# TensorE reads the two halves of its moving operand in turn

## The chip, the cores and the metric

The kernel runs on one core of a Trainium2 chip. The metric is the device time of one execution in microseconds (us). Before the change it is 957.76 us, the median of 3 runs (957.65 to 957.94).

## The reference

One layer of a pooling mixer with two RMS norms, on 4096 frames of 1024 channels in float32:

```
normed = rms_norm(h, norm_w)
u, gate = split(normed @ in_w, 2)                 # in_w: 1024 x 2048
pooled = [trailing_mean(u_g, window_g) for 4 groups, windows 2/4/8/16] - u
mixed = einsum('bsgc,gcd->bsgd', pooled, group_w) + group_b
y = mixed * scale * silu(gate)
h = h + y @ out_w                                  # out_w: 1024 x 1024
out = rms_norm(h, final_norm_w)
```

## The kernel before

The group maps are folded into the input weights at the start (`fold`, line 364), so that two large products are left: the input product, in two passes `a` and `b` over the halves of the weights, and the output product `o`. Each is done with Strassen's scheme in Winograd's form: a 2 x 2 block product by seven products P1 to P7 instead of eight. The order of the seven is `ORDER_IN` and `ORDER_OUT` (lines 32 and 33).

Each float32 operand is split in two parts by `split` (line 153): ScalarE rounds it to fp32r, VectorE subtracts that from the operand, and the rest is the second part. `mm3` (line 554) then issues three fp32r matmuls for one product of 128 x 128 by 128 x 512: first part by first, first by second, second by first. The three add up in one PSUM bank of 512 float32 columns.

There are 56 steps of the input product (2 passes, 4 blocks of 1024 frames, 7 products), each with 48 matmuls (`product_in`, line 563), and 56 of the output product (8 blocks of 512 frames, 7 products), each with 24 (`product_out`, line 584). In `product_in` the stationary operand is a slice of 128 columns of the weights `w[i][h]`, and the moving operand is a row of 512 frames of an activation tile `op`. In `product_out` the activations are stationary and a row of 512 columns of `w[i]` is moving. All matmuls of both go through `mm3`. The last step of all does its second bank as two pieces of 256 columns, the second of them into the bank called "spare", so that the tail can begin earlier.

`evict_in` (line 665) and `evict_o` (line 861) read the banks. After P1 ScalarE copies the banks into another set of banks, on which later products accumulate. The other products are copied to SBUF by ScalarE (in one case through a SiLU) or added to an SBUF tile by VectorE. In the output part the SBUF tile is the row of `x` to which the product is added; `finish` (line 763) then takes squares, the inverse root and the final weights, and stores the rows. In the last block the same is done in pieces by `square_part`, `early_half`, `late_factor`, `late_scalar` and `late_vector` (lines 797 to 859).

Eight banks serve as two sets of four in the input part and as four pairs that rotate in the output part. Loads run three to four steps ahead, forming and splitting of operands one to two steps ahead (lines 1132 to 1141 and the loop from line 1156). In the head, before the first product, TensorE runs eight constant products (line 978), the folds (line 373) and the spreading of the norm factors over a bank (line 432). `spread_rs` (line 424) reads its own bank 7 with a step of 128 words in the source (lines 442 to 445).

Of the kernel before, what the change touches and what calls it, by code (L numbers as in the profile page):

```python
# [12 lines left out]
AF = mybir.ActivationFunctionType  # L13
ALU = mybir.AluOpType
# [4 lines left out]
H = 512  # L19
# [9 lines left out]
EPS = 1e-6  # L29
# [31 lines left out]
def kernel(  # L61
# [66 lines left out]
    def take(pattern="p (a b) -> p a b", pool=None, **sizes):  # L128
        sizes = sizes or {"a": 2}
        if pool is None:  # L130
            spare = len(vt.free) > keep[0] or not st.free
            pool = vt if spare and vt.age() < st.age() else st
        return pool.take(lambda t: t[:, 0:D].rearrange(pattern, **sizes))

    def take_v():
        return vt.take(lambda t: t.rearrange("p (a b) -> p a b", a=2))
# [4 lines left out]
    def add(dst, a, b):  # L141
        nc.vector.tensor_tensor(out=dst, in0=a, in1=b, op=ALU.add)  # L142
# [4 lines left out]
    def mul(dst, a, b):  # L147
        nc.vector.tensor_tensor(out=dst, in0=a, in1=b, op=ALU.mult)  # L148

    def copy(dst, src, func=AF.Copy):  # L150
        return nc.scalar.activation(dst, src, func)  # L151
# [107 lines left out]
    parts, t2 = {}, {}  # L259
# [291 lines left out]

    def mm3(ps, lt, r, start, stop):

        for n, (a, b) in enumerate(((lt[0], r[0]), (lt[0], r[1]), (lt[1], r[0]))):
            latest[0] = nc.tensor.matmul(  # L557
                ps, a, b, start=start and n == 0, stop=stop and n == 2, skip_group_check=True
            ).ins
# [24 lines left out]
    def product_out(i, t, sets, last):  # L584
        ps = sets[bank_of[i]]
        for j in range(2):
            rows = slice(j * P, (j + 1) * P)
            size = H // 2 if last and j == 1 else H
            for c in range(0, H, size):
                cols = slice(c, c + size)  # L590
                dst = sets["spare"] if c else ps[j]
                for k in range(4):
                    wk = w[i][k // 2]
                    mm3(
                        dst[:, cols],
                        (t[:, 0, k, rows], t[:, 1, k, rows]),
                        (wk[:, 0, k % 2, cols], wk[:, 1, k % 2, cols]),
                        (i in (P1, P7) or c > 0) and k == 0,
                        k == 3,
                    )  # L600


# [59 lines left out]
    def cells(us, lo=0):  # L662
        return [us[c // 2][:, c % 2, lo:] for c in range(4)]

    def evict_in(b, q, i, sets):
        ps = sets[bank_of[i]]
        last = None
        if i == P1:
            for c in range(len(copied), 4):
                last = copy(sets["y"][c], ps[c])  # L670
            copied.clear()
        elif i == P2:
            ev["11"] = [take() for _ in range(2)]
            for c, u in enumerate(cells(ev["11"])):
                last = copy(u, ps[c], AF.Silu)
        elif i == P6:
            ev["21"] = [take() for _ in range(2)]
            for c, u in enumerate(cells(ev["21"])):
                last = copy(u, ps[c])
        elif i == P7:  # L680
            ev["22"] = [take_v() for _ in range(2)]
            for c, u in enumerate(cells(ev["22"], HIST)):
                last = copy(u, ps[c])
        elif i == P5:
            for c, u in enumerate(cells(ev["22"], HIST)):
                add(u, ps[c], u)
        elif i == P4:
            for c, u in enumerate(cells(ev["21"])):
                add(u, ps[c], u)
            for u in ev["21"]:  # L690
                copy(u, u, AF.Silu)
        else:
            ev["12"] = [take_v() for _ in range(2)]
            for c, u in enumerate(cells(ev["12"], HIST)):
                last = copy(u, ps[c])
        if last is not None:
            evicted[0] = last.ins

# [82 lines left out]
    partial = {}  # L781
# [3 lines left out]
    def column():  # L785
        k = next(free_columns)
        return columns[:, k : k + 1]

    def mean_part(ss, before):

        ms = column()
        partial["added"] = nc.vector.tensor_scalar(
            out=ms, in0=ss, scalar1=1.0 / D, scalar2=before, op0=ALU.mult, op1=ALU.add
        ).ins
        return ms

    def square_part(u):
        ss = column()
        partial["square"] = nc.scalar.activation(  # L799
            partial["junk"][:, 0, 0 : u.shape[1]], u, AF.Square, accum_out=ss  # L800
        )
        return ss

    def early_half(half, j, n):

        u = hs[NBO - 1][half, j][:, n]
        partial[half, j] = mean_part(square_part(u), EPS)
        mul(u, u, fw[0][:, n])

    def late_factor(half, j, parts):  # L810
# [26 lines left out]
    def late_scalar(half, j, n, rs, queue):  # L837
        u = hs[NBO - 1][half, j]
        with tc.issue_after(partial["last"].ins):
            partial["last"] = nc.scalar.activation(u[:, 1 - n], u[:, 1 - n], AF.Copy, scale=rs)  # L840
        partial["sent"] = queue.dma_start(
            out=out[row_of(NBO - 1, half, j), (1 - n) * H : (2 - n) * H], in_=u[:, 1 - n]
        ).ins
# [17 lines left out]
    def evict_o(b, i, sets):  # L861
        ps = sets[bank_of[i]]
        final = b == NBO - 1
        if final and i == P7:
            partial["junk"] = take()
        factors = []
        for j in range(2):
            if i == P1:
                copy(sets["y"][j], ps[j])
                continue  # L870
            half, n = {P7: (1, 1), P6: (1, 0), P2: (0, 0), P5: (1, 1), P4: (1, 0), P3: (0, 1)}[i]
            u = hs[b][half, j][:, n]
            last = final and i in (P4, P3)
            parts = 2 if last and i == P3 and j == 1 else 1
            for p in range(parts):
                c = slice(p * (H // parts), (p + 1) * (H // parts))
                src = sets["spare"] if p else ps[j]
                partial["added"] = nc.vector.tensor_tensor(  # L878
                    out=u[:, c], in0=src[:, c], in1=u[:, c], op=ALU.add
                ).ins  # L880
                if last:
                    with tc.issue_after(partial["last"].ins) if p else nullcontext():
                        partial["part", p] = square_part(u[:, c])
                if parts == 2 and p == 0:
                    partial["last"] = partial["square"]
                    late_scalar(half, 0, n, factors[0], nc.sync)
            if last:
                factors.append(late_factor(half, j, parts))
                if i == P4 and j == 1 or i == P3 and j == 0:
                    if i == P4:  # L890
                        late_scalar(half, 0, n, factors[0], nc.scalar)
                        late_vector(half, 0, n, factors[0])
                        partial["waiting"] = (half, 1, n, factors.pop())
                    else:
                        rows = partial.pop("waiting")
                        late_scalar(*rows, nc.scalar)
                        late_vector(*rows)
        if final and i == P3:
            late_vector(half, 0, n, factors[0])
            late_scalar(half, 1, n, factors[1], nc.scalar)  # L900
            late_vector(half, 1, n, factors[1], 2)
        if final and i == P5:
            u = hs[b][0, 1][:, 1]
            add(u[:, H // 2 :], ps[1][:, H // 2 :], u[:, H // 2 :])
        if final and i in (P2, P5):
            for j in range(2):
                early_half(half, j, n)
        elif not final and i in (P4, P3):
            finish(b, 1 if i == P4 else 0)
# [37 lines left out]
    def run(n, between=None, behind=None):  # L947
        kind, b, i = steps[n]
        sets = sets_of(kind, b)
        if kind == "o":  # L950
            product_out(i, split_up.pop(n), sets, n == len(steps) - 1)
            evict_o(b, i, sets)
        else:
            product_in(i, split_up.pop(n), sets, i == P1, between, behind)
            evict_in(b, 0 if kind == "a" else 1, i, sets)
# [125 lines left out]
    s = xs[0]  # L1081
# [74 lines left out]
    for n in range(2, len(steps)):  # L1156
        kind, b, i = steps[n]
# [49 lines left out]
        if kind in ("a", "b"):  # L1207
# [7 lines left out]
            if kind == "b" and b == NB - 1 and i == P3:  # L1215
                f = take("p (a b) -> p a b", a=2)
                nc.sync.dma_start(
                    out=f.rearrange("p a b -> p (a b)"), in_=final_w.partition_broadcast(P)
# [54 lines left out]
```

## Time and profile before

| | |
|---|---|
| median of 3 runs | 957.76 us (957.65 to 957.94) |
| the profiled execution | 957.33 us, span 955.5 us |
| mean granted TensorE clock | 0.998 |
| HBM read and written | 115.45 MB and 60.83 MB |
| matmul records | 4212, of which 4044 on line 557 |

In the profile PE is TensorE's matmuls, PEld its weight loads, which run beside them, DVE is VectorE, ACT ScalarE, POOL GpSimd and SP SyncE. A group of instructions shows its line, engine and operation, what it writes and reads with the shapes, the count, then the busy time in us and the mean ns of one, then the idle time of the engine before them and what ended it. A row of the timeline shows a start, a length and a number of instructions merged into it; the length reaches from the first start to the last end. A row of windows shows the stretch, its length and the busy time of PE, PEld, DVE, ACT and POOL with counts, then the granted clock, the share of the DMA engines and GB/s. A row of waits shows who waited for whom, the total in us, how often, and the longest.

### The profile page before, as it was taken

What the parts mean: (1) busy time and instruction counts of PE and PEld (TensorE: products, weight loads), DVE (VectorE), ACT (ScalarE), POOL (GpSimd) and SP (SyncE); (2) the same over time, 40 slices, a digit from 0 to 9 for tenths busy, and PEclk for the clock granted to TensorE, in tenths of its full rate; (3) what the DMA queues carried; (4) which work ended last, traced back from release to release, by engine and by line L of the source; (5) the groups of instructions that cost most, each with busy time, mean ns of one, the idle gap of its engine ahead of it and who ended that gap; (6) DMA issues with size and microseconds to landing.
All of it is one profiled execution on the core that took longest, in us unless ns stands there. A gap on an engine that the chain in (4) does not pass through costs nothing.

```text
span 955.5 us, 11153 instructions
## 1 busy us (share of the span) xinstructions
PE 947.0 (99%) x4212; PEld 784.2 (82%) x4212; DVE 731.5 (77%) x807; ACT 455.8 (48%) x685; POOL 46.4 (5%) x118
## 2 busy tenths in 40 slices
PE   9999999999999999999999999999999999999997
PEld 7888888888888888888888888888888888888886
DVE  3897984894895994796695699499977667676665
ACT  6968457447345455345345435552433424324333
POOL 0023001000000000000000000000101101001010
PEclk9999999999999999999999999999999999999999
DMA  9976666557566644018415724645746536456022
GB/s 344 402 292 241 229 239 196 193 215 245 208 243 218 211 143 143 11 57 295 154 45 195 263 93 140 221 150 172 255 155 210 165 119 222 119 188 210 32 89 89
DMA packets 67573, 177.01 MB, mean 185 GB/s; under 512 B 6720, under 2 KB 24512, under 8 KB 67520
## 3 DMA queue, kind: packets, MB, share of 16 engines
q1 hardware_dynamic: 61616, 156.37, 47.6%
q10 hardware_dynamic: 4176, 13.65, 3.7%
q0 software_dynamic: 1728, 6.29, 1.7%
q8 instruction: 33, 0.54, 0.2%
q14 instruction: 20, 0.16, 0.1%
HBM read 115.45 MB, written 60.83 MB: 184 GB/s over the span
## 4 chain that ended last, share of the span: by engine, by line
PE 95%; DMA 3%; ACT 1%; DVE 0%; SPq 0%; issue 0%; DVEq 0%; ACTq 0%
PE bank L557 94%; DMA early<-in_wut 2%; DMA st<-in_x 1%; PE bank L373 0%; ACT early L407 0%; ACT op L151 0%; ACT w L151 0%; ACT st L799 0%; ACT bank L151 0%; ACT vt L407 0%; PE bank L432 0%; SPq L342 0%; SPq L352 0%; DVE st L878 0%; ACT early L389 0%
## 5 line engine op out<-in xcount | busy, mean ns | idle before, releaser
L557 PE MATMUL bank<-op,w 128*128 128x512 f32 x2688 | 610.5, 389 | 0.2 <-ACT w L223 0.2
L557 PEld LDWEIGHTS bank<-op,w 128*128 128x128 f32 x2688 | 504.4, 188 | 105.5 <-ACT w L223 0.6
L557 PE MATMUL bank<-w,op 128*128 128x512 f32 (+1 forms) x1356 | 305.0, 387 | 0.0
L557 PEld LDWEIGHTS bank<-w,op 128*128 128x128 f32 x1356 | 253.1, 188 | 51.9
L151 ACT ACTIVATE op<-st 128x1024 fp32r<-128x1024 f32 x126 | 132.7, 1057 | 181.3 <-PE bank L557 169.3
L145 DVE TENSOR_TENSOR op<-st,op 128x1024 fp32r<-128x1024 f32 x126 | 152.8, 1219 | 70.9 <-ACT op L151 70.7
L142 DVE TENSOR_TENSOR vt<-vt 128x1028 f32<-128x1028 f32 (+6 forms) x72 | 87.4, 1228 | 0.1
L151 ACT ACTIVATE vt<-bank 128x512 f32<-128x512 f32 x102 | 59.5, 596 | 47.1 <-PE bank L557 46.6
L151 ACT ACTIVATE op<-vt 128x1024 fp32r<-128x1024 f32 x40 | 42.3, 1059 | 72.0 <-PE bank L557 72.0
L878 DVE TENSOR_TENSOR st<-bank,st 128x512 f32<-128x512 f32 x60 | 41.2, 688 | 39.5 <-PE bank L557 39.5
L145 DVE TENSOR_TENSOR st<-st,st 128x1024 f32<-128x1024 f32 x38 | 46.0, 1218 | 14.5 <-DMA st<-wvd 9.1
L145 DVE TENSOR_TENSOR op<-vt,op 128x1024 fp32r<-128x1024 f32 x40 | 48.8, 1221 | 10.1 <-ACT op L151 10.0
L151 ACT ACTIVATE bank<-bank 128x512 f32<-128x512 f32 x48 | 27.9, 581 | 38.9 <-PE bank L557 31.6
L193 POOL TENSOR_SCALAR oms<-oss 128x2 f32<-128x2 f32 x14 | 9.7, 690 | 639.5 <-ACT st L768 635.0
L878 DVE TENSOR_TENSOR vt<-bank,vt 128x512 f32<-128x512 f32 (+1 forms) x37 | 24.9, 673 | 16.1 <-PE bank L557 16.0
L142 DVE TENSOR_TENSOR vt<-bank,vt 128x512 f32<-128x512 f32 (+1 forms) x55 | 36.0, 678 | 0.3 <-PE bank L557 0.2
L145 DVE TENSOR_TENSOR w<-st,w 128x1024 fp32r<-128x1024 f32 x20 | 24.1, 1220 | 11.9 <-ACT w L151 11.7
L642 DVE SCALAR_TENSOR_TENSOR vt<-vt,vt 128x1024 f32<-128x1024 f32 x24 | 29.2, 1217 | 0.0
L151 ACT ACTIVATE w<-st 128x1024 fp32r<-128x1024 f32 x20 | 20.9, 1058 | 16.1 <-PE bank L557 15.4
L148 DVE TENSOR_TENSOR st<-st,st 128x1024 f32<-128x1024 f32 (+1 forms) x19 | 21.7, 1162 | 6.9 <-DMA st<-rd 6.2
L647 DVE SCALAR_TENSOR_TENSOR vt<-vt,colt,vt 128x512 f32<-128x512 f32 x38 | 26.8, 744 | 0.0
L772 DVE SCALAR_TENSOR_TENSOR st<-st,ors,st 128x1024 f32<-128x1024 f32 x17 | 21.4, 1281 | 6.1 <-POOL ors L211 6.1
(121 smaller groups left out, 506.4 us busy)
## 6 DMA issues: line engine op xcount, KB each, us to landing
st<-in_x SPq DMA_DIRECT2D x33, 512.0 KB, 4.6
st<-sd SPq DMA_DIRECT2D x29, 512.0 KB, 5.0
st<-in_xt SPq DMA_DIRECT2D x25, 512.0 KB, 6.5
vt<-in_x SPq DMA_DIRECT2D x24, 512.0 KB, 4.7
sd<-st ACTq DMA_DIRECT2D x19, 512.0 KB, 3.4
yd<-vt SPq DMA_DIRECT2D x19, 512.0 KB, 3.0
st<-yd SPq DMA_DIRECT2D x19, 512.0 KB, 3.8
out<-st SPq DMA_DIRECT2D x17, 512.0 KB, 4.1
```

The costliest lines, as they stand in the source:

```text
L142: nc.vector.tensor_tensor(out=dst, in0=a, in1=b, op=ALU.add)
L145: return nc.vector.tensor_tensor(out=dst, in0=a, in1=b, op=ALU.subtract)
L148: nc.vector.tensor_tensor(out=dst, in0=a, in1=b, op=ALU.mult)
L151: return nc.scalar.activation(dst, src, func)
L193: nc.gpsimd.tensor_scalar(out=ms, in0=ss, scalar1=1.0 / D, scalar2=EPS, op0=ALU.mult, op1=ALU.add)
L557: latest[0] = nc.tensor.matmul(ps, a, b, start=start and n == 0, stop=stop and n == 2, skip_group_check=True).ins
L642: nc.vector.scalar_tensor_tensor(out=s[:, :, at : at + H], in0=s[:, :, at : at + H], scalar=1.0 / win, in1=v[:, :, HIST:], op0=ALU.mult, o ...
L647: nc.vector.scalar_tensor_tensor(out=sg[:, j], in0=s[:, j, at : at + H], scalar=bias_c[2 * grp + j], in1=sg[:, j], op0=ALU.add, op1=ALU.mult,)
L772: nc.vector.scalar_tensor_tensor(out=us[j], in0=us[j], scalar=rs[:, j : j + 1], in1=fw[0], op0=ALU.mult, op1=ALU.mult,)
L878: partial["added"] = nc.vector.tensor_tensor(out=u[:, c], in0=src[:, c], in1=u[:, c], op=ALU.add).ins
```

## The change

A bank's 512 columns are held in the order 0, 256, 1, 257, ..., 255, 511. `woven` gives the moving operand in that order, as a pattern of 256 by 2 with an inner step of 256 words, so each matmul writes its bank as contiguously as before and reads its moving operand from the first and the second half in turn. `plain` reads a bank back in the old order, with a step of two words, and `halved` gives an SBUF tile the matching shape. The columns of the last step's pieces are now counted in pairs: each piece has 128 columns of either half. The copies from bank to bank after P1 keep the new order. The stationary operands, the folds and the spreading are not touched.

```
+    def halved(ap):
+        return ap.rearrange("p (s a) -> p s a", s=2)
+    def woven(ap):
+        return ap.rearrange("p (s a) -> p a s", s=2)
+    def plain(bank):
+        return bank.rearrange("p (a s) -> p s a", s=2)
-    def mm3(ps, lt, r, start, stop):
+    def mm3(bank, lt, r, start, stop, cols=slice(0, H // 2)):
+        ps = bank.rearrange("p (a s) -> p a s", s=2)[:, cols]
+        r = [woven(b)[:, cols] for b in r]
         for n, (a, b) in enumerate(((lt[0], r[0]), (lt[0], r[1]), (lt[1], r[0]))):
             latest[0] = nc.tensor.matmul(
                 ps, a, b, start=start and n == 0, stop=stop and n == 2, skip_group_check=True
...
-            size = H // 2 if last and j == 1 else H
-            for c in range(0, H, size):
-                cols = slice(c, c + size)
+            size = H // 4 if last and j == 1 else H // 2
+            for c in range(0, H // 2, size):
                 dst = sets["spare"] if c else ps[j]
                 for k in range(4):
                     wk = w[i][k // 2]
                     mm3(
-                        dst[:, cols],
+                        dst,
                         (t[:, 0, k, rows], t[:, 1, k, rows]),
-                        (wk[:, 0, k % 2, cols], wk[:, 1, k % 2, cols]),
+                        (wk[:, 0, k % 2], wk[:, 1, k % 2]),
                         (i in (P1, P7) or c > 0) and k == 0,
                         k == 3,
+                        slice(c, c + size),
                     )
...
-                last = copy(u, ps[c], AF.Silu)
+                last = copy(halved(u), plain(ps[c]), AF.Silu)
...
-                add(u, ps[c], u)
+                add(halved(u), plain(ps[c]), halved(u))
...
-            partial["junk"][:, 0, 0 : u.shape[1]], u, AF.Square, accum_out=ss
+            halved(partial["junk"][:, 0])[:, :, 0 : u.shape[2]], u, AF.Square, accum_out=ss
...
-                c = slice(p * (H // parts), (p + 1) * (H // parts))
-                src = sets["spare"] if p else ps[j]
+                c = slice(p * (H // 2 // parts), (p + 1) * (H // 2 // parts))
+                src = plain(sets["spare"] if p else ps[j])[:, :, c]
+                dst = halved(u)[:, :, c]
                 partial["added"] = nc.vector.tensor_tensor(
-                    out=u[:, c], in0=src[:, c], in1=u[:, c], op=ALU.add
+                    out=dst, in0=src, in1=dst, op=ALU.add
                 ).ins
...
-            add(u[:, H // 2 :], ps[1][:, H // 2 :], u[:, H // 2 :])
+            late = halved(u)[:, :, H // 4 :]
+            add(late, plain(ps[1])[:, :, H // 4 :], late)
```

More of the change, by code (lines that the diff above doesn't have):

```diff
@@ L678, in evict_in @@
             for c, u in enumerate(cells(ev["21"])):
-                last = copy(u, ps[c])
+                last = copy(halved(u), plain(ps[c]))
         elif i == P7:
@@ L682, in evict_in @@
             for c, u in enumerate(cells(ev["22"], HIST)):
-                last = copy(u, ps[c])
+                last = copy(halved(u), plain(ps[c]))
         elif i == P5:
             for c, u in enumerate(cells(ev["22"], HIST)):
-                add(u, ps[c], u)
+                add(halved(u), plain(ps[c]), halved(u))
         elif i == P4:
             for c, u in enumerate(cells(ev["21"])):
-                add(u, ps[c], u)
+                add(halved(u), plain(ps[c]), halved(u))
             for u in ev["21"]:
@@ L694, in evict_in @@
             for c, u in enumerate(cells(ev["12"], HIST)):
-                last = copy(u, ps[c])
+                last = copy(halved(u), plain(ps[c]))
         if last is not None:
@@ L806, in early_half @@
         u = hs[NBO - 1][half, j][:, n]
-        partial[half, j] = mean_part(square_part(u), EPS)
+        partial[half, j] = mean_part(square_part(halved(u)), EPS)
         mul(u, u, fw[0][:, n])
@@ L882, in evict_o @@
                     with tc.issue_after(partial["last"].ins) if p else nullcontext():
-                        partial["part", p] = square_part(u[:, c])
+                        partial["part", p] = square_part(dst)
                 if parts == 2 and p == 0:
```

## The prediction

> **What bounds the kernel now.** I read the busy totals first, then the chain of waits, the waits of TensorE, and a stretch in the middle.
>
> ```profile
> span 955.5 us, 11153 instructions
> PE 947.0 (99%) x4212; PEld 784.2 (82%) x4212; DVE 731.5 (77%) x807; ACT 455.8 (48%) x685; POOL 46.4 (5%) x118
> PEclk9999999999999999999999999999999999999999
> 57.59 888.62 PE bank L557 x3919
> 37.70:953.50 915.80, 911.15 (x4032) 754.36 (x4030) 710.19 (x778) 427.85 (x640) 46.02 (x113) 1.00 0.51 178
> ```
>
> TensorE is busy for 99% of the span, at the full granted clock in every slice. The fourth line, from the chain of work that ended last, says that 888.62 us of it are 3919 matmuls of line 557 in one piece. The last line, a stretch without the head, has 911.15 of 915.80 us busy.
>
> ```profile
> PE bank L373 <- DMA early<-in_group_w: 0.8, 1, 0.8
> PE bank L978 <- PEq L1258: 0.8, 1, 0.8
> PE bank L373 <- DMA early<-in_wut: 0.3, 1, 0.3
> PE bank L557 <- ACT w L223: 0.2, 1, 0.2
> ```
>
> These are all the waits of TensorE in total: 2.1 us, of which 0.2 belong to line 557. No eviction, buffer or transfer holds it. The time is therefore the number of matmuls times the distance between two of them. These rows give both.
>
> ```profile
> L557 PE MATMUL bank<-op,w 128*128 128x512 f32 x2688 | 610.5, 389 | 0.2 <-ACT w L223 0.2
> L557 PE MATMUL bank<-w,op 128*128 128x512 f32 x1332 | 302.1, 389 | 0.0
> L557 PE MATMUL bank<-w,op 128*128 128x256 f32 x24 | 3.0, 283 | 0.0
> L557 PEld LDWEIGHTS bank<-op,w 128*128 128x128 f32 x2688 | 504.4, 188 | 105.5 <-ACT w L223 0.6 <-DVE op L145 0.4
> ...
> 399.76 4.47 PE L557 MATMUL bank<-op,w 128*128 128x512 f32 x19
> ...
> 13.77 3.40 PE L373 MATMUL bank<-w,w 128*128 128x256 f32 x27
> ```
>
> The 389 ns of one is its whole passage; neighbours overlap. The distance comes from the timeline: 19 matmuls take 4.47 us, the last of them its full 0.389, so (4.47 - 0.389) / 18 = 0.2267 us for 512 columns. The 27 fp32r matmuls of 256 columns in the head, with 283 ns for the last, give (3.40 - 0.283) / 26 = 0.1199 us. The difference, 0.1068 us for 256 columns, is 0.417 ns per column, and 0.2267 - 0.2136 = 0.013 us per matmul are left that do not depend on the columns. The 0.417 ns is the speed at which moving words now arrive, every one beside its neighbour.
>
> **The change, part by part.** No instruction is added, removed or moved: the same matmuls, weight loads, evictions and DMAs in the same order. What differs is the order of addresses within them.
>
> *The moving reads.* Each of the 4020 matmuls of 512 columns and the 24 of 256 now reads word 0, word 256, word 1, word 257 and so on: every word lies about 1 KiB from the one before it (in the last step's pieces too). No read of SBUF in this trace steps like that, so the price is bounded by rows.
>
> ```profile
> L978 PE MATMUL bank<-const-bfloat16-1.0 128*128 128x512 bf16 x8 | 3.2, 572 | 0.8 <-PEq L1258 0.8
> L151 ACT ACTIVATE op<-st 128x1024 fp32r<-128x1024 f32 x126 | 132.7, 1057 | 181.3 <-PE bank L557 169.3 <-DVE st L148 8.8 <-issue 2.0
> L145 DVE TENSOR_TENSOR op<-st,op 128x1024 fp32r<-128x1024 f32 x126 | 152.8, 1219 | 70.9 <-ACT op L151 70.7
> ```
>
> The cheap end is nothing, or less (the gain is priced among the rivals). For the dear end: the other engines take a 4-byte word from SBUF in 1057 / 1024 = 1.03 ns (ScalarE) and 1219 / 1024 = 1.19 ns (VectorE). TensorE takes one in 0.417 ns, 2.5 to 2.9 times as fast. That makes it likely, though not shown, that its reader fetches neighbours together; when neighbours in time are never neighbours in place, it fetches once per word. If single words came at VectorE's pace, a matmul would cost 512 x (1.19 - 0.417) = 0.396 us more: 4020 x 0.396 + 24 x 0.198 = 1597 us, ending at 957.3 + 1597 = 2554 us. If it fetches pairs today, one word per fetch doubles the column to 0.835 ns. A row near that is TensorE's own slowest stream, the eight constant products at the start: 3.2 us / 8 / 512 = 0.78 ns per column. I take 0.835 ns, because TensorE's own row lies beside it and VectorE's time holds more than a read. The matmul then costs 0.2136 us more, 0.440 in all.
>
> [...]
>
> *The evictions.* They read PSUM with a step of two words. For ScalarE there is a row with a much longer step: the copy of bank 7 after the eight products of line 432 reads with a step of 128 words (lines 442 to 445).
>
> ```profile
> 22.68 1.19 PE L432 MATMUL bank<-w,hl 128*128 128x128 f32 x8
> 23.91 0.60 ACT L151 ACTIVATE st<-bank 128x512 f32<-128x512 f32 x1 [1.64 <-PE bank L432]
> L151 ACT ACTIVATE vt<-bank 128x512 f32<-128x512 f32 x102 | 59.5, 596 | 47.1 <-PE bank L557 46.6
> L878 DVE TENSOR_TENSOR st<-bank,st 128x512 f32<-128x512 f32 x60 | 41.2, 688 | 39.5 <-PE bank L557 39.5
> L878 DVE TENSOR_TENSOR vt<-bank,vt 128x512 f32<-128x512 f32 x35 | 24.1, 688 | 16.0 <-PE bank L557 16.0
> L142 DVE TENSOR_TENSOR vt<-bank,vt 128x512 f32<-128x512 f32 x54 | 35.6, 683 | 0.3 <-PE bank L557 0.2
> L142 DVE TENSOR_TENSOR st<-bank,st 128x512 f32<-128x512 f32 x10 | 6.7, 682 | 0.1
> 650.00:940.00 290.00, 290.00 (x1281) 240.22 (x1280) 211.69 (x243) 101.27 (x146) 22.23 (x70) 1.00 0.46 154
> ```
>
> That copy takes 0.60 us, the contiguous ones 0.596, so ScalarE's evictions cost nothing more. For VectorE no row has a step; its 60 + 35 + 54 + 10 = 159 evictions of 512 columns lie between no change and twice 0.69 us, at most 110 us in all. I take nothing, by ScalarE's row. The cover is TensorE's stream: with today's pace VectorE would go from 731.5 to 841 busy us; in the output part, the last line above, 95 of these evictions would bring it from 211.7 to 277 of 290 us, which still fits but tightly. If some evictions were then late, the next product's bank or operand would be late, and I allow up to 10 us for it. If the matmuls double, the cover doubles too. Near the end two of VectorE's are of 256 columns:
>
> ```profile
> 947.66 0.42 DVE L878 TENSOR_TENSOR vt<-bank,vt 128x256 f32<-128x256 f32 x1
> ...
> 949.18 0.41 DVE L878 TENSOR_TENSOR vt<-bank,vt 128x256 f32<-128x256 f32 x1
> ...
> L557 PE MATMUL bank<-op,w x2688: 387/389/578, 32.7 to 643.9; 128*128 128x512 f32 x192
> ```
>
> Only the second comes after the last matmul, so the tail grows by under 0.5 us even if it doubles.
>
> *Sum.* The profiled execution took 957.33 us, 1.8 more than its span, and lies 0.4 under the median of 957.76. The head, up to the first matmul of line 557 at 32.7 us (last line above), and the tail keep their time. 957.3 + 4020 x 0.2136 + 24 x 0.1068 = 957.3 + 858.7 + 2.6 = **1819 us**.
>
> **The rivals.**
>
> 1. *The hops are free* (a buffer in TensorE's reader holds both halves' words). For it: each half by itself is still read in order, so every fetched block is used up within a few columns. Against it: the reader must then serve two streams at 0.417 ns per word, and nothing here shows that it can. Time: 957.8; with late VectorE evictions up to 968.
>
> [...]
>
> 2. *Faster* (the other side): each matmul carries 0.013 us that its columns do not explain, and a weight load of 188 ns runs under it. If that is the moving stream held up by the weight load at one place of SBUF, reading two places in turn could take the delay away.
>
> ```profile
> 24.62 3.62 PE L373 MATMUL bank<-early,early 128*128 128x256 f32 x16
> L373 PE MATMUL bank<-early,early 128*128 128x256 f32 x96 | 21.7, 382 | 1.1 <-DMA early<-in_group_w 0.8 <-DMA early<-in_wut 0.3
> ```
>
> For it: the float32 products of the head, 48 in the code and 96 in the trace, stand (3.62 - 0.379) / 15 = 0.2161 us apart (0.379 is this shape's usual length); if each record streams its 256 columns twice, at half the word rate, only 0.0024 us is left, so the 0.013 is not fixed for all products. Against it: the distance is the same 0.2267 at any place and load, and a slower fetch would outweigh it. It decides from the point where hopping costs less than 0.02 ns a column. Price: 4020 x (0.2267 - 0.2161) = 43 us, so 915.
>
> 3. *A fetch brings four words*: then single words run at a quarter of the rate, three times 0.2136 more per matmul: 957.3 + 3 x 861.3 = 3541 us. For it: full-rate fp32 with a wide block needs the fewest fetches. Against it: 1.67 ns per word would be slower than VectorE's 1.19, which holds two operands and a write.
>
> 4. *A part of the hops hides*: somewhere between free and double; half of it is 1388 us.
>
> 5. *Between double and VectorE's pace*: 1819 to 2554, say 2190 us.
>
> **How the numbers follow.** Half rate 0.36; free 0.25, of which 0.19 within 0.2% (about what a measurement of this kernel can tell from no change) and 0.06 beyond it through evictions; faster 0.10; quarter rate 0.13; partly hidden 0.11; above double 0.05. Half rate leads because reading neighbours in pairs is the least that the pace ratio of the rows asks for. Faster is 0.10, same 0.19, slower 0.36 + 0.06 + 0.13 + 0.11 + 0.05 = 0.71. The range leaves out the quarter rate and half of the faster case (below 935): 935 to 2554, which holds 0.36 + 0.25 + 0.05 + 0.11 + 0.05 = 0.82. The likeliest case's own range is 1790 to 1850.
>
> **What would show it.** Right: the distance between matmuls of line 557 is 0.43 to 0.45 us, the 24 short ones double as well, the head's line 373 keeps 0.1199, and the granted clock stays at 1.00; a lower clock at the same distance would mean a throttle instead of reads. ScalarE's evictions stay near 0.60 us and VectorE's at 0.68 to 0.69. TensorE waits for nothing new, and VectorE's share falls to about 731.5 / 1817 = 40%. The forecast is wrong if the distance stays at 0.2267 (free) or nears 0.216 (faster), or if VectorE's evictions lengthen and TensorE's waits grow beyond 2 us.

## The result and the profile after

| | before | after |
|---|---|---|
| median | 957.71 us (4 runs, 957.65 to 957.94) | 924.66 us (4 runs, 922.32 to 926.86) |
| ratio, with its 95% interval | | 0.9654 (0.9622 to 0.9686) |
| the profiled execution, and its span | 957.33 us, 955.5 us | 926.72 us, 924.9 us |

The changed kernel is 3.5% faster. The forecast was 1819 us, and its range began at 935. Among all the executions that follow, one, of the version with words 4 apart, was slow (1248.68 us at a granted clock of 0.72), and its ratio leaves it out. The page of the kernel after, its totals and the row of the granted clock:

```profile
span 924.9 us, 11163 instructions
PE 907.7 (98%) x4212; PEld 791.0 (86%) x4212; DVE 729.1 (79%) x807; ACT 449.4 (49%) x685; POOL 48.9 (5%) x118
PEclk9999999999999999999999999999999999999999
```

Each engine has as many instructions as before, but TensorE is busy for 39 us less. A piece of the timeline after, in the middle, gives the distance between two matmuls (line 570 is line 557 of before):

```profile
398.69 4.48 PE L570 MATMUL bank<-op,w 128*128 128x512 f32 x20
```

With 0.379 us for the last one (the groups' rows give 379 to 381 ns of one), it is (4.48 - 0.379) / 19 = 0.2158 us, against 0.2267 before. That is 10.8 ns less on each matmul. 4020 matmuls of 512 columns make it 43.5 us, but the profiled execution gained only 30.6. The waits of TensorE after show where the rest went:

```profile
PE bank L570 <- DVE op L145: 5.5, 4, 2.5
PE bank L570 <- ACT bank L151: 1.5, 1, 1.5
PE bank L570 <- ACT w L223: 1.3, 1, 1.3
```

Line 557 had waited 0.2 us in all; line 570 waits 8.3. Summed over the trace's start times from the first product on, the distances longer than the usual one are 13.9 us over it after and 1.1 before. 43.5 - 12.8 = 30.7 us, which is the gain to 0.1 us. The first of the large waits, TensorE's timeline after, then the same stretch before:

```profile
111.71 8.15 PE L570 MATMUL bank<-op,w 128*128 128x512 f32 x37
122.33 9.94 PE L570 MATMUL bank<-op,w 128*128 128x512 f32 x37 [2.47 <-DVE op L145]
```

```profile
111.67 20.56 PE L557 MATMUL bank<-op,w 128*128 128x512 f32 x90
```

VectorE's timeline after says why the operand was late:

```profile
108.57 1.22 DVE L145 TENSOR_TENSOR op<-st,op 128x1024 fp32r<-128x1024 f32 x1
109.70 6.89 DVE L148 TENSOR_TENSOR st<-st,vt 128x1024 f32<-128x1024 f32 x6
116.51 2.35 DVE L145 TENSOR_TENSOR st<-st,st 128x1024 f32<-128x1024 f32 x2
118.78 1.22 DVE L145 TENSOR_TENSOR vt<-st,st 128x1024 f32<-128x1024 f32 x1
119.92 1.22 DVE L145 TENSOR_TENSOR st<-st,st 128x1024 f32<-128x1024 f32 x1
121.06 2.35 DVE L145 TENSOR_TENSOR op<-st,op 128x1024 fp32r<-128x1024 f32 x2
```

TensorE began the second product of the block at 119.5, and from its second matmul on, at 119.7, it needed the two splits of 121.06 (`op<-st,op`). Ten other operations stand between them and the split before: six normalisations (line 148) and four subtractions for the third product. VectorE runs without a pause through all of them. The order is the same before, at nearly the same time:

```profile
120.19 2.34 DVE L145 TENSOR_TENSOR op<-st,op 128x1024 fp32r<-128x1024 f32 x2
```

There the first of the two splits ended at 121.4, and TensorE came to that matmul at 122.1, by the trace's times: a slack of 0.7 us. A step lasted 48 x 0.2267 = 10.9 us before and lasts 10.4 now. After eight such steps, and the waits among them, TensorE comes to the same matmul 2.4 us sooner than before, while the split ends 0.9 us later, at 122.3. The slack covered only 0.7 of that.

The evictions after, of ScalarE and VectorE, against 596, 688, 688 and 683 ns before:

```profile
L151 ACT ACTIVATE vt<-bank 128x512 f32<-128x512 f32 x102 | 58.1, 593 | 31.3 <-PE bank L570 31.0
L892 DVE TENSOR_TENSOR st<-bank,st 128x512 f32<-128x512 f32 x60 | 41.2, 692 | 26.4 <-PE bank L570 26.2
L892 DVE TENSOR_TENSOR vt<-bank,vt 128x512 f32<-128x512 f32 x35 | 24.0, 688 | 11.7 <-PE bank L570 11.4
L142 DVE TENSOR_TENSOR vt<-bank,vt 128x512 f32<-128x512 f32 x54 | 35.6, 685 | 0.0
```

In these groups reading a bank with a step of two words costs neither engine more than 4 ns of one.

### The profile page after: what moved, and what is told of

It is laid out like the page before. It is cut to its first block, busy times and chain, and to the rows that moved or that the text cites. A ratio compares the mean times of both kernels' runs of the same rounds, so it can differ in the third digit from the quotient of the medians.

```text
span 924.9 us, 11163 instructions
## 1 busy us (share of the span) xinstructions
PE 907.7 (98%) x4212; PEld 791.0 (86%) x4212; DVE 729.1 (79%) x807; ACT 449.4 (49%) x685; POOL 48.9 (5%) x118
## 4 chain that ended last, share of the span: by engine, by line
PE 58%; DVE 24%; DMA 10%; ACT 4%; issue 3%; POOL 1%; SPq 0%; DVEq 0%; ACTq 0%; POOLq 0%
PE bank L570 56%; DVE vt L142 6%; DVE op L145 5%; DVE st L145 3%; PE bank L373 2%; DVE st L148 2%; DVE vt L655 1%; DMA st<-in_out_w 1%; DMA rd<-rs 1%; DVE st L142 1%; DMA wod<-st 1%; DVE vt L660 1%; DMA st<-rd 1%; ACT op L151 1%; DMA st<-wvd 1%
## 5 line engine op out<-in xcount | busy, mean ns | idle before, releaser
L570 PE MATMUL bank<-op,w 128*128 128x512 f32 x2688 | 586.0, 381 | 8.4 <-DVE op L145 5.5
L570 PEld LDWEIGHTS bank<-op,w 128*128 128x128 f32 x2688 | 509.7, 190 | 83.9 <-DVE op L145 7.6
L570 PE MATMUL bank<-w,op 128*128 128x512 f32 (+1 forms) x1356 | 290.3, 377 | 0.0
L193 POOL TENSOR_SCALAR oms<-oss 128x2 f32<-128x2 f32 x14 | 11.7, 839 | 613.9 <-ACT st L781 609.5
L151 ACT ACTIVATE w<-st 128x1024 fp32r<-128x1024 f32 x20 | 20.9, 1057 | 12.5 <-PE bank L570 10.8
L151 ACT ACTIVATE vt<-vt 128x1024 f32<-128x1024 f32 (+1 forms) x12 | 11.8, 987 | 30.8 <-DVE vt L142 30.8
```

The costliest lines, as they stand in the source:

```text
L193: nc.gpsimd.tensor_scalar(out=ms, in0=ss, scalar1=1.0 / D, scalar2=EPS, op0=ALU.mult, op1=ALU.add)
L570: latest[0] = nc.tensor.matmul(ps, a, b, start=start and n == 0, stop=stop and n == 2, skip_group_check=True).ins
```

## The experiments

### The orders of reading by themselves

Two questions were open: what sets the price of an order, and why the new one is cheaper than the plain one. The first kernel holds nothing but matmuls, most of them on one fp32r tile: 24 in order to begin with, then 40 of each order, such as these (`m` is 512 words, `wt` the weights):

```
for n in range(40):
    w_, m_ = wt, m.rearrange("p (s a) -> p a s", s=2)
    nc.tensor.matmul(shape(banks[n % 8], m_), w_, m_, start=True, stop=True, skip_group_check=True)
```

> This kernel computes none of the reference: it only runs 26 groups of 40 matmuls back to back, fp32r 128x128 by 128x512 where nothing else is said, which differ in the order in which the moving operand (or the weights) is read; the number is the distance between neighbours. The kernel before has 226.7 ns in order, the changed one 215.8 with halves in turn, and both should come back here. Theory A (the weight load and the moving stream meet at one place of SBUF): in order with one weight column for all, or with weights far away, falls to 215.8; with halves in turn the weights do not matter. Theory B (the moving stream alone: neighbouring words read at full speed cost a fixed 11 ns): the weights change nothing in order (226.7 throughout), while every pattern whose neighbours in time are not neighbours in place gives 215.8, the step of 2 and 2 apart in turn too; pairs or runs of 4 in turn stay at 226.7. Theory C (the form of the pattern: one free dimension takes another path than two): runs of 64 in turn give 215.8 too, and the step of 2 in one dimension stays at 226.7. bf16 in order is 215.8 by A (fewer bytes to meet) and by B; if it is 226.7 the 11 ns have nothing to do with 4-byte words. A half-rate price of single words, as forecast, would show in some stepped pattern as about 440.

Some rows of its timeline, each with 40 matmuls: in order (136), halves in turn (140), pairs in turn (144), a step of two, evens and then odds (160), quarters in turn (172), words 4 apart in turn (180), bf16 in order (224) and bf16 halves in turn (228):

```profile
12.58 9.23 PE L136 MATMUL bank<-mv,wt 128*128 128x512 f32 x40
21.64 8.79 PE L140 MATMUL bank<-mv,wt 128*128 128x512 f32 x40
30.28 13.76 PE L144 MATMUL bank<-mv,wt 128*128 128x512 f32 x40
...
72.73 18.29 PE L160 MATMUL bank<-mv,wt 128*128 128x512 f32 x40
...
126.54 11.51 PE L172 MATMUL bank<-mv,wt 128*128 128x512 f32 x40
...
157.35 8.84 PE L180 MATMUL bank<-mv,wt 128*128 128x512 f32 x40
...
248.62 8.81 PE L224 MATMUL bank<-bm,bw 128*128 128x512 bf16 x40
257.26 19.54 PE L228 MATMUL bank<-bm,bw 128*128 128x512 bf16 x40
```

The length less one matmul's own, over 39, is the distance: (9.23 - 0.389) / 39 = 0.2267 us in order, (8.79 - 0.379) / 39 = 0.2157 with halves in turn. The groups' distances, as means over the trace's start times without each group's first nine matmuls (the granted clock is 1.00 through all groups of this set and of the two that follow):

| order of the 512 words | ns |
|---|---|
| in order | 226.7 |
| halves in turn; or words 4 apart in turn (0 4 1 5 2 6 3 7) | 215.8 |
| words 2 apart in turn (0 2 1 3); runs of 64 in turn | 227.0 |
| runs of 8; runs of 4; pairs in turn | 243.4; 250.1; 340.0 |
| quarters; eighths in turn | 283.3; 486.7 |
| step of 2; of 4; of 8 | 453.4; 461.3; 431.1 |
| in order from an odd word | 236.6 |
| in order, weights far away | 226.7 |
| one and the same word 512 times | 218.7 |
| 256 columns in order; halves in turn | 120.0; 111.6 |
| bf16 in order; halves in turn | 215.8; 484.5 |

Theory C falls: runs of 64 have the same form of pattern as the halves and stay at 227.0. Theory B falls in its second half: a step of two is not at 215.8 but costs double (453.4), words 2 apart stay at 227.0, and pairs, which were to stay, cost half as much again (340.0). Theory A is not borne out: neither far weights (226.7) nor, at a noisy 228.9, one weight column for all brought a stream in order to 215.8. What the table shows instead is that single words in turn from two places have no price (215.8), be the places 1 KiB or four words (16 bytes) apart, while two words apart brings nothing (227.0), and four or eight places are dear (283.3 and 486.7). That the reader simply holds two places is not shown: pairs from the same two places cost 340.0.

A second set asked whether the 10.8 ns sit in the weight load, in the stream column by column or in something fixed. Two lines in turn, in the expectation, are single words in turn from two places, such as the halves or words 4 apart, which came to 215.8 above; no run shows that TensorE reads in lines.

> Computes none of the reference: 22 groups of 40 matmuls, as in the first set of patterns. What is open: where the 10.8 ns between in order (226.7) and two lines in turn (215.8) sit. Theory A' (the weight load, 128 columns, takes read slots from a stream in order, which has none to spare): with 64 weight columns in order comes to 221, with 32 to 218.5, and with weights at a step of 8 two lines in turn still show 215.8 to 218. Theory B' (a fixed cost at the start of each stream in order): 64 and 32 weight columns stay at 226.7, 384 columns in order are 173.3 against 162.5 in turn, and 256 with 32 weight columns 120.0 against 109.2. [...] Distance does not matter to either: 8, 32 and 257 apart in turn give 215.8, if the reader simply holds two lines; if it matters where the two lines lie, one of them differs. [...] bf16 8 apart in turn (two lines) about 216 if it holds two lines for bf16 as for fp32r, and near 484 as the halves did if it does not.

| second set | in order, ns | halves in turn, ns |
|---|---|---|
| 512 columns, 128 weight columns | 226.7 | 215.8 |
| 512 columns, 64; 32 weight columns | 229.8; 231.7 | (not run); 215.8 |
| 512 columns, weights at a step of 8 words | 245.4 | 240.5 |
| 384 columns, 128 weight columns | 173.3 | 162.5 |
| 256 columns, 32 weight columns | 113.3 | 109.2 |

Words 8, 32 and 257 apart in turn gave 215.8, and halves from an odd word 216.6. Theory A' falls: 64 and 32 weight columns do not shorten the stream in order (229.8 and 231.7 against 226.7). Nor is the difference in proportion to the columns: 384 columns save 10.8 ns as 512 do. Theory B' holds at these two lengths with full weight loads, but not at 256 columns (8.4 ns in the first set), and not at 32 weight columns, where the difference is 15.9 ns with 512 columns and 4.1 with 256. For bf16, words 8 apart in turn, two places as well, cost 485.6, pairs of the halves in turn 271.2, and only words 4 apart, 8 bytes, stayed at 215.8. That two places in turn are free is therefore not so for every type.

A third set asked on which side of a stream the time lies.

> Computes none of the reference: 15 groups of 40 matmuls, as in the first two sets. Open: the fixed 10.8 ns of an fp32r stream in order, whatever its length. Theory E (its own stream is longer by 10.8 ns, at its end or inside): in a sequence of in order and halves in turn by turns, the distance behind the one in order is 226.7 and behind the other 215.8; with bf16 by turns the one behind fp32r in order is 226.7 and behind bf16 215.8. Theory F (it starts late, whatever went before): the 10.8 ns then stand ahead of the stream in order, so behind the halves in turn and behind bf16. Theory G (two fp32r streams in order meet, the end of one and the first line of the next): neither distance is 226.7 in the sequences by turns, both are 215.8. Two places by turns, other starts on a whole line (word 4) and two far rows stay at 226.7 by all three; a start at word 2 lies between 226.7 and the 236.6 of an odd start. 448 columns: 200.0 in order, 189.2 in turn.

Where a stream in order and one with halves in turn alternate, the distance behind the one in order was 231.7 ns and behind the other 215.0. The longer one is where theory E has it, though 5 ns longer than it said; F and G fall. Alternating with bf16, the pair took 460 ns with the stream in order and 447 with halves in turn, but the single distances there (422 and 38, 408 and 39) say nothing about the sides. That neighbouring matmuls read the same words is not the cause either: 512 words from two places by turns stayed at 226.7. Of the other expectations, a start at word 2 (233.4) and 448 columns with halves in turn (189.2) came as said; a start at word 4, a whole line by the expectation, missed, 231.6 instead of 226.7, and so did 448 columns in order, 202.7 instead of 200.0. So an fp32r stream in order is longer by itself, but not by the same at every length: by 10.8 ns at 512 and at 384 columns, 13.5 at 448, 8.4 at 256. What in the reader makes it so stays open.

### The output product alone, and the input product alone

```
-        ps = bank.rearrange("p (a s) -> p a s", s=2)[:, cols]
-        r = [woven(b)[:, cols] for b in r]
+        if weave:
+            ps = bank.rearrange("p (a s) -> p a s", s=2)[:, cols]
+            r = [woven(b)[:, cols] for b in r]
+        else:
+            ps = bank[:, 2 * cols.start : 2 * cols.stop]
+            r = [b[:, 2 * cols.start : 2 * cols.stop] for b in r]
```

`weave` is false in `product_in` for the first kernel and in `product_out` for the second, and the evictions of that part are those of before.

> The changed order in the output product alone (1320 + 24 matmuls); the input product, its banks and its evictions as before. If the gain is 10.8 ns per matmul and all of what was given back belongs to the input part, then 957.5 - 1344 x 0.0108 = 943.0 us, with TensorE's waits as before (2 us) and no distance of 427. If the evictions with a step of two cost VectorE time that counts, it stays above 946.

Measured: 943.47 us, ratio 0.9849 (0.9828 to 0.9871), and 943.0 was expected. TensorE waits for 0.7 us at the products.

> The changed order in the input product alone (2688 matmuls), the output product as before. 957.5 - 2688 x 0.0108 = 928.4 us if nothing is given back; with the 11 to 13 us of late operands that the changed kernel shows before 280 us, 937 to 942 us, and the late operands are there at the same places. If those came from the output part or from chance, it is nearer 929.

Measured: 934.83 us, ratio 0.9759 (0.9738 to 0.9780), between the two expectations. Its waits of TensorE:

```profile
PE bank L574 <- DVE op L145: 4.5, 3, 2.3
```

The two longest distances stand at 119.1 and 266.8 us, near two of the changed kernel's places (119.5 and 270.0), and all the long ones together are 6.6 us over the usual ones. 957.9 - 2688 x 0.0108 + (6.6 - 1.1) = 934.4 us, within 0.2 us of its profiled execution. What was given back belongs to the input part; how much of it varies, since the other late operands of the changed kernel are missing here.

### The split for the second product first

```
-        if kind == "a" and b > 0 and i == P1:
-            normalize_a2(b)
+        first = kind == "a" and b > 0 and i == P1
         normal = kind == "a" and step(n + 2)[2] in (P1, P2)
-        if n > 2 and not normal:
+        if n > 2 and not normal and not first:
             form(n + 2)
         advance("split", n, split_step, split_reach)
+        if first:
+            with tc.issue_after(latest_split[0]):
+                normalize_a2(b)
+                form(n + 2)
```

> The changed kernel with one order changed: in the first step of each block after the first, VectorE finishes the split for the second product before it normalises and forms the operands of the third. Theory S (the operand of the second product is late because eight VectorE operations, 9.8 us, are queued ahead of its split in a step that now has 10.4 us): the late operands at 119, 196, 260 and 270 us go, and with them the half-speed distances of 427 ns behind two of them: 914 to 917 us. Theory T (VectorE is simply full there, whatever the order): the lateness moves to the third product and the time stays at 922 to 927.

Measured: 916.81 us, ratio 0.9576 (0.9558 to 0.9593). This is below both kernels. Its VectorE and TensorE timelines at the same place:

```profile
112.99 1.22 DVE L145 TENSOR_TENSOR op<-st,op 128x1024 fp32r<-128x1024 f32 x1
114.12 1.41 DVE L660 SCALAR_TENSOR_TENSOR vt<-vt,colt,vt 128x512 f32<-128x512 f32 x2
115.45 1.22 DVE L142 TENSOR_TENSOR vt<-vt 128x1028 f32<-128x1028 f32 x1
116.59 1.22 DVE L145 TENSOR_TENSOR op<-st,op 128x1024 fp32r<-128x1024 f32 x1
117.73 4.62 DVE L148 TENSOR_TENSOR st<-st,vt 128x1024 f32<-128x1024 f32 x4
```

```profile
111.65 11.82 PE L570 MATMUL bank<-op,w 128*128 128x512 f32 x54
124.53 7.82 PE L570 MATMUL bank<-op,w 128*128 128x512 f32 x35 [1.06 <-ACT bank L151]
```

The two splits now end at 117.8 us, before TensorE wants them, and eight of the ten operations follow, four normalisations first. VectorE's work is the same, so theory T falls: it is the order, not the amount. One wait of 1.06 us is new at 123 us, on a copy between banks; the later ones at 196, 260, 270 and 568 us are gone. The control is the kernel before with the same order:

> The kernel before, with the split for the second product put ahead of the normalising and forming for the third, as in the faster version of the changed kernel. If that order only takes back what the shorter steps made late, it is worth nothing here, as no operand was late: 957 to 958.5 us. If it is a gain of its own, it is below 956.

Measured: 958.02 us, ratio 0.9998 (0.9987 to 1.0009). The order is worth nothing where nothing was late; it only lets the shorter matmuls count.

### Other orders in the whole kernel

The column order 0, 4, 1, 5, ... in the version with the split first; the last step's pieces and the evictions follow it:

```
-        return ap.rearrange("p (s a) -> p a s", s=2)
+        return ap.rearrange("p (k s a) -> p k a s", s=2, a=4)
```

> The faster version (split for the second product first), with another order of the columns: 0, 4, 1, 5, 2, 6, 3, 7, then the next eight. If what counts is that two places of 16 bytes are read in turn, wherever they lie, the distance is 215.8 and the time 916 to 919 us, as with the halves. If it needs the two halves, 1 KiB apart, the distance is 226.7 and the time 957.

Measured: 916.98 us, ratio 0.9572 (0.9553 to 0.9591), the same as with the halves. Two neighbouring places of 16 bytes do as well as two that are 1 KiB apart (916.98 and 916.81 us).

Four quarters in turn in the changed kernel (`s=4` in `halved`, `woven`, `plain` and `mm3`):

> The changed kernel with four quarters in turn instead of two halves. From the patterns alone (283.3 ns against 226.7 in order): 957.5 + 4020 x 0.0566 + 24 x 0.028 = 1186 us, slower than before, with nothing late. If the reader can hold more than two places once the kernel's other traffic spaces its reads, or if the price in the kernel is another one, it is not within 1175 to 1195.

Measured: 1184.46 us, ratio 1.2364 (1.2339 to 1.2389). The timeline:

```profile
399.63 20.56 PE L570 MATMUL bank<-op,w 128*128 128x512 f32 x72
```

(20.56 - 0.448) / 71 = 0.2833 us, the distance of the pattern by itself (0.448 us is the length of one of these matmuls). The pattern set prices this kernel to 2 us.

## Why the prediction was wrong

**What bounds the kernel** was right: the number of matmuls times their distance, with the long distances added, accounts for before, after and all variants to about 2 us.

**The evictions** were right at no cost (at most 4 ns of one), VectorE's included, for which no row had shown a step.

**The moving reads** are where it failed, at the sentence "when neighbours in time are never neighbours in place, it fetches once per word", and with it the 0.835 ns per column. No run shows how many words a fetch brings; the pace of TensorE against the other engines, from which it was argued, does not show it either. Nor does it say that a place once left is lost, and with two places the patterns show that it is not: words of the halves, or 8, 32 or 257 apart, in turn all come to 215.8 ns for 512 columns, less than the 226.7 in order. The doubled price exists, at a step of 2 (453 ns against the forecast 440) and in eighths (487), and with quarters the price begins (283.3). The working treated every hop alike, although its own first rival said what was different here: two streams, each still in order.

The row beside which 0.835 was chosen, the constant products at 0.78 ns per column, is no price of reading. Their shortest, median and longest length, before:

```profile
L978 PE MATMUL bank<-const-bfloat16-1.0 x8: 381/634/634, 0.8 to 3.6; 128*128 128x512 bf16 x8
```

Five of the seven distances between them are 426 or 427 ns, the last is 273, and the last product takes 381 ns. 426 or 427 is also the distance of the kernel after's matmuls where the granted clock falls to 0.52 (last section), and the one at which the opening stream of the first pattern set starts, which is in order and then settles at 227 (24 matmuls in 7.4 us, where 227 throughout would make 5.6). In the traces before and after, the distance in the head falls where the record of the granted clock begins, with 1.0 (3.4 us). bf16 in order by itself runs at 215.8. So the slow start of TensorE was taken for a slow stream.

**The faster rival**, with a chance of 0.10, was the one. Its size was right: 0.2161 us was read from the float32 products of the head, 0.2158 came. Its cause is not supported: it blamed the weight load, and weights far away (226.7), or 64 or 32 weight columns in place of 128 (229.8 and 231.7), did not shorten the stream in order (226.7). The float32 products were read in order themselves, so nothing tied their pace to the new order, and that the size came true is luck.

**The sum of that rival**, 915 us, was short by some 10 because it let the whole gain through. The forecast asked what the longer path would cover and never what the shorter one would uncover. The shorter steps brought TensorE 2.4 us sooner to a split that had 0.7 us of slack, with ten VectorE operations queued ahead of it. The version with the split first reaches 916.81.

**The range** began at 935 by cutting the faster case in half; the measured 924.66 lies in the half left out.

## What to carry to other kernels

An access order has no price by its step alone: measure the very order in a loop of 40 matmuls, because halves, quarters and a step of two came to 215.8, 283.3 and 453.4 ns. When the bound engine gets faster, look for the operand whose producer had the least slack, and move its last operation ahead of work that is due later, as the split first did for another 8 us. A distance that is longer than its columns explain, such as 226.7 where 213.6 is streaming by the slope between 256 and 512 columns, is worth a question even where nothing waits.

## What was not expected of the hardware

The same order that fp32r likes (halves in turn, 215.8 ns against 226.7) is dear for bf16 (484.5 against 215.8 ns) and for full float32 (256 columns, 273.3 against 215.8 for each record). Stepped weights slow the matmul as well: at a step of 8 words 245.4 in order, against 226.7.

A late operand cost more than its wait. Two stretches of the kernel after, the first right behind the wait of 2.47 us, the second a little later:

```profile
122.80:126.20 3.40, 3.40 (x10) 2.65 (x9) 3.40 (x4) 0.00 (x0) 0.00 (x0) 0.52 0.79 284
127.00:131.00 4.00, 4.00 (x20) 3.52 (x19) 4.00 (x5) 1.48 (x2) 0.00 (x0) 1.00 0.51 206
```

The granted clock (the third figure from the end) fell to 0.52 for 3.4 us, and ten matmuls began where sixteen would have; the same happened behind the wait at 270 us (0.54 from 272.8 to 276.2). 14 distances of 426 or 427 ns in the trace are 14 x 0.211 = 3.0 us of the 12.8 given back. The input product alone had a wait of nearly the same size (2.3 us) at 119.1 us without it. The waits ahead of the dips were 2.47 and 2.02 us; what set the dips off is not shown. That the dips are also why the changed kernel's runs lie at 922 and at 927 us (mean granted clock 0.996 and 0.995) was not tried.
